# The odd token groups' gating tiles in the place of the units' first weight block, and the projection's first weight sum built there

## The chip, the cores and the metric

The kernel runs on one core of a Trainium2 chip. The metric is the time of one execution on the device in microseconds (us), the median of several runs. Engines have in-order queues: TensorE (PE in the rows) multiplies, VectorE (DVE) and ScalarE (ACT) do elementwise work, GpSimd (POOL) and SyncE (SP) issue loads and stores. A load that adds to what its target holds (an accumulating load) is issued by GpSimd.

## What is computed

A decoder layer with three token mixers, for 512 tokens of width 2048. What matters here is its second half:

```python
y_a = gmlp_branch(a_u, a_v, a_z, ...) @ w_branch_a      # u * (spatial mix of layer_norm(v)) * silu(z)
y_b = dsa_branch(...) @ w_branch_b
y_m = memory_branch(...) @ w_branch_m
merged = (sigmoid(g_a) * y_a + sigmoid(g_b) * y_b + sigmoid(g_m) * y_m)
x = x + merged @ w_out                                  # 512 x 2048 times 2048 x 2048
```

## The kernel before, in words

Every float32 product is made of three matmuls on parts: a weight tile `raw` is cast to `whi` by ScalarE (line 136), `wlo` is the rest, by VectorE (line 137), and lines 160 to 162 multiply hi by hi, hi by lo and lo by hi. A weight chunk is 256 rows by 512 columns (512 KB); its three matmuls for two or four groups of 128 tokens are 12 or 24 matmuls. Three buffers each for `whi` and `wlo` and four for `raw` set how far ahead weights come.

The gate columns g_m, g_b, g_a (and v, z before them) and the output projection are computed in **units** of 1024 columns by Strassen's scheme: seven products of half-size blocks, in the order A11, S1, S2, A12, S3, A22, N4, with weight sums in the tiles `a` (four buffers of the pool `hold`) and `b` (another four). Results wait in `ev` (four buffers) to be stored to DRAM as `kept_*`.

When the last gate unit is over, the pools `hold` and `ev` close, and `cpool` opens in their place, with the branch a operand `ya0`, `ya1` and the tiles `odd0`, `odd1`. The **gating** of branch a goes through the four groups of 128 tokens (c = 0 to 3): it loads the factors v, u, z of a group (line 938), takes statistics (989), scales (994, 996), multiplies u by z (998), mixes on TensorE (1005) and transposes into `ya` (1016). Even groups use the large pool's tiles, odd ones `odd0` and `odd1`. It runs as a task: pieces of it are issued between the weight chunks of the **branch products**, which go m, b, a for the column groups (512 columns each) 0 and 1, then m, b, a for 2 and 3. At the end of each, line 1119 multiplies the result in PSUM by its gate, which frees the bank, and 1121 adds. After branch a, `merged` is transposed (1035, 1036).

The **projection** begins with a unit of its own (`first_output_unit`), with the products in the order A11, S3, S1, S2, A12, A22, N4. Its left operands come from `merged`: A11 and S3 from the left half (`left_half`, which uses `odd1` for its differences), S1, S2 and N4 from the right half (`right_half(j)`, j = 0 and 1: column groups 2 and 3). S3's weights are B12 + B22, built in `b` by a plain load by SyncE (`b12_22`, line 1164) and an accumulating load (1174); S1's are B11 + B12, built so in `a` (1164, 1179). The pools `hold` and `ev` are open again for this, in the place of `cpool`. The second unit is the general `strassen`.

The scheduler that records the program sets each engine's order; the source gives dependences and priorities.

Of the kernel before, what the change touches and what calls it, by code (L numbers as in the profile page):

```python
# [59 lines left out]
def hybrid_block(ctx: ExitStack, tc: tile.TileContext, a, out):  # L60
# [717 lines left out]
    def held(tag):  # L778
        return pools["hold"].tile([P, CK, 512], F32, tag=tag, name=tag)
# [61 lines left out]
    def strassen(w, c0, finished, placing=None, after={}, ops=ops, before_last=None):  # L841

        wv = w.rearrange("(k p) c -> p k c", p=P)
        def load(to, kh, ch, k):
            SP.dma_start(to, wv[:, kh * 8 + k:kh * 8 + k + CK, c0 + ch * 512:c0 + ch * 512 + 512])
            return to
# [12 lines left out]
        def b11(k):  # L859
            va[k] = load(held("a"), 0, 0, k)  # L860
            parts = split_pair(va[k])
            vb[k] = load(held("b"), 0, 1, k)
            add(va[k], vb[k])
            if k == 8 - CK and placing:
                placing()
            return parts
# [68 lines left out]
    def factors_load(c, new):  # L935
        uvz[c] = two = new()
        for t, i, name in ((two[0], 0, "v"), (two[1], 0, "u"), (two[1], 1, "z")):
            G.dma_start(t[:, i, :], kept[name][:, c, :])
# [35 lines left out]

    stage = opened(("cpool", 1))
    y_of["a"] = tuple(pools["cpool"].tile([P, 8, T], F32R, tag=f"ya{n}", name=f"ya{n}") for n in range(2))
    odd8 = lambda tag="odd1": pools["cpool"].tile([P, 2, 1024], F32, tag=tag, name=tag)
    odd_two = lambda: (odd8("odd0"), odd8("odd1"))

    def gating():  # L980
        for c in range(NT):
            if c + 1 < NT and c % 2 == 0:
                factors_load(c + 1, odd_two)
# [56 lines left out]
    gops, raws, s1_first = {}, {"S2": [], "N4": []}, []  # L1040
# [28 lines left out]
    def right_half(j, s1, s2, n4):  # L1069

        a11, a21, a12, a22 = (quarter(n, j) for n in ("a11", "a21", "a12", "a22"))
        raws["S2"].append(s2)
        raws["N4"].append(n4)
        V.tensor_tensor(s1, a21, a22, op=OP.subtract)
        if j == 0:
            s1_first.append(s1)
        else:
            eighth("S1")
            for i, t in enumerate((s1_first[0], s1)):
                into("S1", i, t)  # L1080
                yield 1220
        V.tensor_tensor(s2, s1, a11, op=OP.subtract)
        V.tensor_tensor(n4, a12, s2, op=OP.add)
        yield 2440
        if j == 0:
            sixteen("A12")
            sixteen("A22")
        into("A12", j, a12)
        into("A22", j, a22)
        yield 2440  # L1090
# [8 lines left out]
    for name, cg in [(name, cg) for first in (0, 2) for name in "mba" for cg in (first, first + 1)]:  # L1099
# [26 lines left out]
        if name == "a":  # L1126
            turning = submit(turned_out(cg))
            if cg == 2:
                kept_sums = odd8("odd0")
                submit(right_half(0, quad(kept_sums[:, 0:1]), quad(kept_sums[:, 1:2]),  # L1130
                                  score_all[:, :1024].rearrange("p (k c) -> p k c", c=256)))
# [3 lines left out]
    stage = opened(("ev", 4), ("hold", 4))  # L1135
    w_out = a["w_out"]

# [20 lines left out]
    def first_output_unit():  # L1158
# [13 lines left out]
        def b12_22(k):  # L1172
            vb[k] = load(held("b"), 0, 1, k)
            G.dma_start(vb[k], block(1, 1, k), accum_op=OP.add)
            return split_pair(vb[k])
# [20 lines left out]
        e1 = ev()  # L1196
        S.copy(e1, x)
# [3 lines left out]
        n4_made = submit(parts_of("N4"))  # L1201
        e7 = ev()
        S.copy(e7, y)
        z = bank()
        block_product(gops["S1"], z, b11_12, budget=bud)
        block_product(gops["S2"], y, b11_12_22, onto=True, budget=bud)
        finish(n4_made)
        V.tensor_tensor(e1, y, e1, op=OP.add)
# [16 lines left out]
    halves = submit(right_half(1, *(quad(ev()) for _ in range(3))))  # L1225
    first_output_unit()
    strassen(w_out, 1024, given_out(1024), ops=gops, before_last=less_x(1024))
    stage.close()
    stage_s.close()
# [35 lines left out]
```

## Time and profile before

| | |
|---|---|
| median of 3 runs | 1845.69 us (1844.81 to 1846.19) |
| the profiled execution | 1846.42 us |
| its span, first to last instruction | 1844.7 us |
| TensorE busy, share of the span | 1804.9 us, 98% |
| VectorE, ScalarE busy | 1244.6 us (67%), 762.2 us (41%) |
| mean granted TensorE clock | 0.991 |
| last gate unit ends, branch products begin | 1374.48 us |
| projection begins (A11, S3, S1, S2) | 1664.65, 1688.04, 1706.00, 1720.13 us |

The span is what the trace shows; the execution's own time has 1.7 us more around it. [...]

### The profile page before, as it was taken

The numbers are of one execution on the slowest core, as the hardware profiler recorded it, in microseconds if no ns is written. First come the engines' busy times: TensorE is split into PE (matmuls) and PEld (weight loads), VectorE is DVE, ScalarE is ACT, GpSimd is POOL, SyncE is SP. The second block draws the span as 40 slices with busy tenths as digits, with TensorE's granted clock in tenths as the row PEclk, the third lists the DMA queues.
The fourth block names the chain that finished last, engine by engine and source line by source line (L and its number), as shares of the span: only waits on it lengthen the run. The fifth ranks groups of instructions, "written<-read, shape, count | busy, mean of one in ns | idle before, by whom it ended". The sixth has DMA issues, their size and how long they took to land.

```text
span 1844.7 us, 21738 instructions
## 1 busy us (share of the span) xinstructions
PE 1804.9 (98%) x8426; PEld 1508.2 (82%) x8426; DVE 1244.6 (67%) x1652; ACT 762.2 (41%) x987; POOL 114.0 (6%) x169
## 2 busy tenths in 40 slices
PE   8999999999999999999999999999998999997998
PEld 6798898888888888888888888888886888885787
DVE  8787679665446556968678686786854653455784
ACT  5744442344334354444544444444442222223443
POOL 8000000000000000000000000000111000002001
PEclk9999999999999999999999999999998999998999
DMA  7744232433332323564645646556676544338754
GB/s 229 281 126 125 70 89 78 126 115 103 94 101 69 126 69 137 184 183 130 202 147 170 185 125 204 150 169 184 221 264 219 172 151 137 126 114 242 202 167 108
DMA packets 129735, 280.95 MB, mean 152 GB/s; under 512 B 9312, under 2 KB 15456, under 8 KB 127584
## 3 DMA queue, kind: packets, MB, share of 16 engines
q1 hardware_dynamic: 111408, 211.98, 37.1%
q0 software_dynamic: 17936, 67.57, 11.2%
q8 instruction: 66, 1.08, 0.2%
q14 instruction: 37, 0.30, 0.1%
q10 hardware_dynamic: 288, 0.02, 0.0%
HBM read 248.08 MB, written 31.46 MB: 152 GB/s over the span
## 4 chain that ended last, share of the span: by engine, by line
issue 52%; PE 37%; DMA 5%; DVE 3%; POOL 2%; ACT 1%; SPq 0%; DVEq 0%; POOLq 0%; ACTq 0%
PE xyz L160 6%; PE xyz L161 6%; PE xyz L162 6%; PE acc L161 3%; PE acc L162 3%; PE acc L160 3%; DMA a<-w_out 2%; PE acc L185 1%; PE acc L186 1%; PE acc L187 1%; DVE wlo L137 1%; DMA raw<-w_branch_m 1%; DVE mTl L256 0%; PE aux L514 0%; PE aux L513 0%
## 5 line engine op out<-in xcount | busy, mean ns | idle before, releaser
L137 DVE TENSOR_TENSOR wlo<-raw,whi 128x1024 fp32r<-128x1024 f32 (+1 forms) x276 | 333.7, 1210 | 315.0 <-ACT whi L136 314.7
L136 ACT CAST whi<-raw 128x1024 fp32r<-128x1024 f32 (+1 forms) x276 | 284.2, 1031 | 556.3 <-PE xyz L162 275.7
L136 ACT CAST whi<-a 128x1024 fp32r<-128x1024 f32 x156 | 164.4, 1055 | 221.3 <-PE xyz L162 205.2
L160 PE MATMUL xyz<-whi,hTh 128*128 128x512 f32 x576 | 224.2, 389 | 0.7 <-ACT b L752 0.7
L137 DVE TENSOR_TENSOR wlo<-a,whi 128x1024 fp32r<-128x1024 f32 x156 | 188.3, 1220 | 53.9 <-ACT whi L136 53.9
L161 PE MATMUL xyz<-wlo,hTh 128*128 128x512 f32 x576 | 224.1, 389 | 0.0
L162 PE MATMUL xyz<-whi,hTl 128*128 128x512 f32 x576 | 224.1, 389 | 0.0
L160 PE MATMUL acc<-whi,hTh 128*128 128x512 f32 (+1 forms) x544 | 203.5, 374 | 0.4 <-ACT b L639 0.4
L161 PE MATMUL acc<-wlo,hTh 128*128 128x512 f32 (+1 forms) x544 | 200.8, 369 | 0.0
L162 PE MATMUL acc<-whi,hTl 128*128 128x512 f32 (+1 forms) x544 | 200.7, 369 | 0.0
L160 PEld LDWEIGHTS xyz<-whi,hTh 128*128 128x128 f32 x576 | 108.1, 188 | 23.5 <-ACT b L752 1.1
L162 PEld LDWEIGHTS xyz<-whi,hTl 128*128 128x128 f32 x576 | 108.1, 188 | 22.5
L161 PEld LDWEIGHTS xyz<-wlo,hTh 128*128 128x128 f32 x576 | 108.1, 188 | 22.4
L160 PEld LDWEIGHTS acc<-whi,hTh 128*128 128x128 f32 x544 | 102.2, 188 | 13.5 <-ACT b L639 0.8
L162 PEld LDWEIGHTS acc<-whi,hTl 128*128 128x128 f32 x544 | 102.1, 188 | 13.4
L161 PEld LDWEIGHTS acc<-wlo,hTh 128*128 128x128 f32 x544 | 102.3, 188 | 12.1
L185 PE MATMUL acc<-hTh,whi 128*128 128x512 f32 x256 | 100.1, 391 | 0.0
L186 PE MATMUL acc<-hTl,whi 128*128 128x512 f32 x256 | 99.7, 390 | 0.0
L187 PE MATMUL acc<-hTh,wlo 128*128 128x512 f32 x256 | 99.7, 389 | 0.0
L137 DVE TENSOR_TENSOR wlo<-b,whi 128x1024 fp32r<-128x1024 f32 x40 | 49.0, 1225 | 65.0 <-ACT whi L136 65.0
L852 DVE TENSOR_TENSOR a<-a,raw 128x1024 f32<-128x1024 f32 x72 | 86.4, 1220 | 0.4
L136 ACT CAST whi<-b 128x1024 fp32r<-128x1024 f32 x40 | 42.1, 1052 | 50.1 <-PE xyz L162 36.8
(363 smaller groups left out, 3530.6 us busy)
## 6 DMA issues: line engine op xcount, KB each, us to landing
raw<-w_in SPq DMA_DIRECT2D x184, 512.0 KB, 3.5
a<-w_in SPq DMA_DIRECT2D x32, 512.0 KB, 4.5
b<-w_in SPq DMA_DIRECT2D x32, 512.0 KB, 3.6
raw<-w_mem_kv SPq DMA_DIRECT2D x31, 512.0 KB, 4.5
raw<-w_out SPq DMA_DIRECT2D x28, 512.0 KB, 4.0
raw<-w_in SPq DMA_DIRECT2D x24, 368.0 KB, 3.1
raw<-w_branch_m SPq DMA_DIRECT2D x16, 512.0 KB, 5.6
raw<-w_branch_b SPq DMA_DIRECT2D x16, 512.0 KB, 3.6
```

The costliest lines, as they stand in the source:

```text
L136: S.copy(hi, src)
L137: V.tensor_tensor(lo, src, hi.bitcast(F32), op=OP.subtract)
L160: PE.matmul(ps, lhsT=lh, rhs=rh, start=first, stop=False, **k)
L161: PE.matmul(ps, lhsT=lh, rhs=rl, start=False, stop=False, **k)
L162: PE.matmul(ps, lhsT=ll, rhs=rh, start=False, stop=last, **k)
L185: PE.matmul(ps[i][:m], lhsT=hi[:, f:f + m], rhs=ah[:, k, :], start=(k == 0), stop=False)
L186: PE.matmul(ps[i][:m], lhsT=hi[:, f:f + m], rhs=al[:, k, :], start=False, stop=False)
L187: PE.matmul(ps[i][:m], lhsT=lo[:, f:f + m], rhs=ah[:, k, :], start=False, stop=(k == ktiles - 1))
L852: V.tensor_tensor(to, to, x, op=OP.add)
```

## The change

The pool with `odd0` and `odd1` opens by itself (`stage_odd`) as soon as the last unit's pools are closed, and stays open to the end. It lies where the first half of `hold`, the four `a` buffers, was; `ya0` and `ya1` lie behind it, where `b` and `ev` were. The loads for token group 1 are issued at once, ahead of the gating task. In the projection `hold` opens first, with `a` alone, at the place of `ya0`, and `ev` at that of `ya1`; `b` is no longer a tag of `hold`: `held_b` gives halves of `odd0` and `odd1`, to the first unit and, by the argument `second`, to the last one. `right_half` is taken apart: `parts_a12_a22(j)` makes the parts of A12 and A22, and `right_sums` makes the sums for S1, S2 and N4 of both halves in the four `ev` buffers, after the last branch product. The two evacuations e1 and e7, which had `ev` buffers early, come later.

```diff
@@ -838,7 +838,8 @@
         for rest in after:
             rest()
 
-    def strassen(w, c0, finished, placing=None, after={}, ops=ops, before_last=None):
+    def strassen(w, c0, finished, placing=None, after={}, ops=ops, before_last=None,
+                 second=lambda k: held("b")):
 
         wv = w.rearrange("(k p) c -> p k c", p=P)
         def load(to, kh, ch, k):
@@ -859,7 +860,7 @@
         def b11(k):
             va[k] = load(held("a"), 0, 0, k)
             parts = split_pair(va[k])
-            vb[k] = load(held("b"), 0, 1, k)
+            vb[k] = load(second(k), 0, 1, k)
             add(va[k], vb[k])
             if k == 8 - CK and placing:
                 placing()
@@ -972,15 +973,17 @@
     stage.close()
 
 
+    stage_odd = opened(("odd", 1))
+    odd8 = lambda tag="odd1": pools["odd"].tile([P, 2, 1024], F32, tag=tag, name=tag)
+    odd_two = lambda: (odd8("odd0"), odd8("odd1"))
+    factors_load(1, odd_two)
     stage = opened(("cpool", 1))
     y_of["a"] = tuple(pools["cpool"].tile([P, 8, T], F32R, tag=f"ya{n}", name=f"ya{n}") for n in range(2))
-    odd8 = lambda tag="odd1": pools["cpool"].tile([P, 2, 1024], F32, tag=tag, name=tag)
-    odd_two = lambda: (odd8("odd0"), odd8("odd1"))
 
     def gating():
         for c in range(NT):
-            if c + 1 < NT and c % 2 == 0:
-                factors_load(c + 1, odd_two)
+            if c == 2:
+                factors_load(3, odd_two)
             vo, uz = uvz.pop(c)
             u, v, o = uz[:, 0, :], vo[:, 0, :], vo[:, 1, :]
             bs = tiny.tile([P, 2, 6], F32, name="bn_s")
@@ -1037,7 +1040,7 @@
             yield 800
 
 
-    gops, raws, s1_first = {}, {"S2": [], "N4": []}, []
+    gops, raws = {}, {"S2": [], "N4": []}
 
     def eighth(name):
         gops[name] = tuple(pools["big"].tile([P, 8, 256], F32R, tag="b8", name=f"g{name}{n}") for n in "hl")
@@ -1066,28 +1069,29 @@
             into("S3", j, s3)
             yield 2440
 
-    def right_half(j, s1, s2, n4):
-
-        a11, a21, a12, a22 = (quarter(n, j) for n in ("a11", "a21", "a12", "a22"))
-        raws["S2"].append(s2)
-        raws["N4"].append(n4)
-        V.tensor_tensor(s1, a21, a22, op=OP.subtract)
-        if j == 0:
-            s1_first.append(s1)
-        else:
-            eighth("S1")
-            for i, t in enumerate((s1_first[0], s1)):
-                into("S1", i, t)
-                yield 1220
-        V.tensor_tensor(s2, s1, a11, op=OP.subtract)
-        V.tensor_tensor(n4, a12, s2, op=OP.add)
-        yield 2440
+    def parts_a12_a22(j):
         if j == 0:
             sixteen("A12")
             sixteen("A22")
-        into("A12", j, a12)
-        into("A22", j, a22)
-        yield 2440
+        for name in ("A12", "A22"):
+            into(name, j, quarter(name.lower(), j))
+            yield 1220
+
+    def right_sums():
+
+        eighth("S1")
+        temps = [quad(ev()) for _ in range(4)]
+        for j, s2, n4 in ((0, temps[1], score_all[:, :1024].rearrange("p (k c) -> p k c", c=256)),
+                          (1, temps[2], temps[3])):
+            a11, a21, a12, a22 = (quarter(n, j) for n in ("a11", "a21", "a12", "a22"))
+            V.tensor_tensor(temps[0], a21, a22, op=OP.subtract)
+            into("S1", j, temps[0])
+            V.tensor_tensor(s2, temps[0], a11, op=OP.subtract)
+            yield 3660
+            V.tensor_tensor(n4, a12, s2, op=OP.add)
+            raws["S2"].append(s2)
+            raws["N4"].append(n4)
+            yield 1220
 
     def parts_of(name):
         eighth(name)
@@ -1126,14 +1130,20 @@
         if name == "a":
             turning = submit(turned_out(cg))
             if cg == 2:
-                kept_sums = odd8("odd0")
-                submit(right_half(0, quad(kept_sums[:, 0:1]), quad(kept_sums[:, 1:2]),
-                                  score_all[:, :1024].rearrange("p (k c) -> p k c", c=256)))
+                submit(parts_a12_a22(0))
     stage.close()
 
 
-    stage = opened(("ev", 4), ("hold", 4))
+    stage = opened(("hold", 4), ("ev", 4))
     w_out = a["w_out"]
+    odds = {}
+
+    def held_b(k):
+
+        if k % (2 * CK) == 0:
+            odds[0] = odd8(f"odd{k // (2 * CK)}")
+        return odds[0][:, k // CK % 2, :].rearrange("p (a c) -> p a c", c=512)
+
 
     tiles_of = lambda t, th, c: t.rearrange("(t p) c -> p t c", p=P)[:, 2 * th:2 * th + 2, c:c + 512]
 
@@ -1170,7 +1180,7 @@
         va, vb = {}, {}
 
         def b12_22(k):
-            vb[k] = load(held("b"), 0, 1, k)
+            vb[k] = load(held_b(k), 0, 1, k)
             G.dma_start(vb[k], block(1, 1, k), accum_op=OP.add)
             return split_pair(vb[k])
 
@@ -1193,18 +1203,18 @@
         bud = 1300
         x = bank()
         block_product(gops["A11"], x, lambda k: split_pair(passing(0, 0, k)), budget=bud)
-        e1 = ev()
-        S.copy(e1, x)
         y = bank()
         block_product(gops["S3"], y, b12_22, budget=bud)
         finish(submit(parts_of("S2")))
         n4_made = submit(parts_of("N4"))
+        z = bank()
+        block_product(gops["S1"], z, b11_12, budget=bud)
         e7 = ev()
         S.copy(e7, y)
-        z = bank()
-        block_product(gops["S1"], z, b11_12, budget=bud)
         block_product(gops["S2"], y, b11_12_22, onto=True, budget=bud)
         finish(n4_made)
+        e1 = ev()
+        S.copy(e1, x)
         V.tensor_tensor(e1, y, e1, op=OP.add)
         e3 = ev()
         V.tensor_tensor(e3, z, e1, op=OP.subtract)
@@ -1222,10 +1232,12 @@
         V.tensor_tensor(e7, z, e7, op=OP.subtract)
         finished(0, 512, e7, ts=slice(0, 2))
 
-    halves = submit(right_half(1, *(quad(ev()) for _ in range(3))))
+    submit(parts_a12_a22(1))
+    submit(right_sums())
     first_output_unit()
-    strassen(w_out, 1024, given_out(1024), ops=gops, before_last=less_x(1024))
+    strassen(w_out, 1024, given_out(1024), ops=gops, before_last=less_x(1024), second=held_b)
     stage.close()
+    stage_odd.close()
     stage_s.close()
     stage_h.close()
 
```

The first place where the order of instructions moves is the end of the last gate unit. On GpSimd (`kept_a<-ev` are stores of that unit's results, `ym` and `yb` the branch operands, `b` tiles of the large pool) there stood before, from the stores on:

```order
L916 DMA kept_a<-ev 128x2x512
L927 DMA yb_10896<-y_b 128x2048
L927 DMA yb_10897<-y_b 128x2048
L916 DMA kept_a<-ev 128x2x512
L927 DMA yb_10896<-y_b 128x2048
L933 DMA b_10894<-kept_m 128x4x512
L916 DMA kept_a<-ev 128x2x512
L927 DMA yb_10897<-y_b 128x2048
L938 DMA odd_10922<-kept_v 128x1024
L938 DMA odd_10923<-kept_u 128x1024
L938 DMA odd_10923<-kept_z 128x1024
L933 DMA b_11081<-kept_b 128x4x512
```

and now:

```order
L917 DMA kept_a<-ev 128x2x512
L939 DMA odd_10768<-kept_v 128x1024
L939 DMA odd_10769<-kept_u 128x1024
L939 DMA odd_10769<-kept_z 128x1024
L928 DMA yb_10904<-y_b 128x2048
L928 DMA yb_10905<-y_b 128x2048
L917 DMA kept_a<-ev 128x2x512
L928 DMA yb_10904<-y_b 128x2048
L934 DMA b_10902<-kept_m 128x4x512
L928 DMA yb_10905<-y_b 128x2048
L917 DMA kept_a<-ev 128x2x512
L934 DMA b_11084<-kept_b 128x4x512
```

The three loads of group 1 moved ahead of the loads of `yb` and of two stores. On VectorE, the work of group 1 (`odd`) stood before behind five splits of weights (the last of N4 and four of branch m) and the evacuation of N4 (909):

```order
L222 TENSOR_TENSOR rs_r<-rs_r,rs_u 128x1
L996 SCALAR_TENSOR_TENSOR b_10664<-b_10664,rs_r,b_10645 128x1024
L137 TENSOR_TENSOR wlo<-raw,whi 128x1024 x3
L909 TENSOR_TENSOR ev<-xyz,ev 128x1024
L137 TENSOR_TENSOR wlo<-raw,whi 128x1024 x2
L989 BN_STATS bn_s<-odd_10922 128x6
L137 TENSOR_TENSOR wlo<-raw,whi 128x1024
L989 BN_STATS bn_s<-odd_10922 128x6
```

and now it begins ahead of the first of them, the split of N4's last chunk:

```order
L992 BN_STATS bn_s<-odd_10768 128x6
L221 TENSOR_SCALAR rs_u<-rs_u 128x1
L992 BN_STATS bn_s<-odd_10768 128x6
L222 TENSOR_TENSOR rs_r<-rs_r,rs_u 128x1
L1001 TENSOR_TENSOR odd_10769<-odd_10769 128x1024
L137 TENSOR_TENSOR wlo<-raw,whi 128x1024
L999 SCALAR_TENSOR_TENSOR b_10664<-b_10664,rs_r,b_10645 128x1024
L137 TENSOR_TENSOR wlo<-raw,whi 128x1024
```

The second place is the start of the projection. SyncE's loads there were, with the last two branch products ahead of them:

```order
L154 DMA raw<-w_branch_b 128x2x512 x8
L154 DMA raw<-w_branch_a 128x2x512 x8
L1164 DMA raw<-w_out 128x2x512 x8
L1164 DMA b<-w_out 128x2x512 x4
L1164 DMA a<-w_out 128x2x512 x4
```

and are now, with `odd_12725` the tile `odd0` and `odd_12772` the tile `odd1`:

```order
L1174 DMA odd_12725<-w_out 128x2x512
L154 DMA raw<-w_branch_a 128x2x512
L154 DMA raw<-w_branch_m 128x2x512 x8
L154 DMA raw<-w_branch_b 128x2x512 x8
L1174 DMA odd_12772<-w_out 128x2x512 x2
L154 DMA raw<-w_branch_a 128x2x512 x8
L1174 DMA raw<-w_out 128x2x512 x6
L1174 DMA a<-w_out 128x2x512 x4
L1174 DMA raw<-w_out 128x2x512 x2
```

The loads of the first sum moved between those of the branch products, those for `a` ahead of the last two single blocks; on GpSimd the accumulating loads (1184) moved likewise, between the gate loads. On VectorE the right half's sums (1087, 1089, 1091) and parts now stand between the splits of A11's last chunk and of S1's first (`wlo<-a`):

```order
L1087 TENSOR_TENSOR ev<-b_11650,b_12478 128x1024
L1089 TENSOR_TENSOR ev<-ev,b_11650 128x1024
L137 TENSOR_TENSOR wlo<-odd_12725,whi 128x1024
L1091 TENSOR_TENSOR score<-b_12478,ev 128x1024
L137 TENSOR_TENSOR A_12515<-b_12641,A_12515 128x1024
L137 TENSOR_TENSOR A_12516<-b_12641,A_12516 128x1024
L137 TENSOR_TENSOR gS1l<-ev,gS1h 128x1024
L137 TENSOR_TENSOR wlo<-odd_12725,whi 128x1024
L137 TENSOR_TENSOR wlo<-odd_12772,whi 128x1024
L1087 TENSOR_TENSOR ev<-b_11803,b_12641 128x1024
L137 TENSOR_TENSOR wlo<-odd_12772,whi 128x1024
L1089 TENSOR_TENSOR ev<-ev,b_11803 128x1024
```

Behind these rows come five more (`gS1l`, the last sum, `gS2l` twice, `wlo<-a`), then `gN4l` twice and the next splits for S1. Before, the first half's three sums had run earlier, beside the last branch product.

## Rows read from the trace of the kernel before

**Rows 1.** The page, part 1: busy time and share of TensorE.

```profile
PE 1804.9 (98%) x8426; PEld 1508.2 (82%) x8426; DVE 1244.6 (67%) x1652; ACT 762.2 (41%) x987; POOL 114.0 (6%) x169
```

**Rows 2.** Waits of TensorE over the span: total, times, longest, us.

```profile
PE xyz L160 <- ACT whi L136: 12.2, 2, 10.4
...
PE xyz L160 <- DVE b L1119: 6.9, 2, 6.4
```

**Rows 3.** Windows: us, busy by engine (PE first, its matmuls in brackets), clock, DMA.

```profile
1374.48:1431.70 57.22, 48.60 (x217) 39.81 (x216) 26.77 (x41) 12.96 (x15) 5.99 (x10) 0.91 0.68 246
...
1575.48:1619.00 43.52, 43.52 (x194) 36.05 (x193) 22.44 (x20) 12.31 (x12) 0.76 (x1) 1.00 0.37 120
...
1664.65:1677.45 12.80, 12.80 (x65) 10.36 (x63) 10.62 (x11) 7.99 (x11) 0.31 (x1) 1.00 0.58 190
...
1677.45:1720.13 42.68, 28.09 (x97) 20.65 (x97) 23.96 (x21) 16.13 (x16) 10.14 (x9) 0.80 1.01 265
```

**Rows 4.** Timeline of TensorE: start, duration, operation, [idle before it <- releaser].

```profile
1406.69 0.79 PE L160 MATMUL xyz<-whi,ym 128*128 128x512 f32 x1 [6.37 <-DVE b L1119]
...
1688.04 0.79 PE L160 MATMUL xyz<-whi,S 128*128 128x512 f32 x1 [10.43 <-ACT whi L136]
```

**Rows 5.** Timeline of VectorE around the last gate unit and the first branch.

```profile
1357.86 1.21 DVE L137 TENSOR_TENSOR wlo<-a,whi 128x1024 fp32r<-128x1024 f32 x1
...
1367.38 0.16 DVE L222 TENSOR_TENSOR rs_r<-rs_r,rs_u 128x1 f32<-128x1 f32 x1
...
1368.78 1.22 DVE L137 TENSOR_TENSOR wlo<-raw,whi 128x1024 fp32r<-128x1024 f32 x1
...
1382.95 1.23 DVE L137 TENSOR_TENSOR wlo<-raw,whi 128x1024 fp32r<-128x1024 f32 x1 [3.81 <-ACT whi L136]
...
1397.00 0.69 DVE L989 BATCH_NORM_STATS2 bn_s<-odd 128x6 f32<-128x512 f32 x1 [9.27 <-DMA odd<-kept_v]
...
1405.42 2.35 DVE L1119 TENSOR_TENSOR b<-b,xyz 128x1024 f32<-128x1024 f32 x2
```

**Rows 6.** The chain that ended last, 1345 to 1450 us: start, us, what.

```profile
1367.12 14.64 DMA raw<-w_branch_m
...
1391.67 5.31 DMA odd<-kept_v
```

**Rows 7.** Line 938, the factor loads: issue to landing, six loads.

```profile
DMA to landing us min/median/max: 4.3/5.5/7.3
```

**Rows 8.** Windows before and in the crowd of loads; DMA share second to last.

```profile
1358.00:1362.00 4.00, 4.00 (x19) 3.32 (x18) 3.93 (x6) 3.41 (x4) 0.67 (x1) 1.00 0.58 236
...
1362.00:1366.00 4.00, 4.00 (x19) 3.32 (x18) 4.00 (x7) 2.32 (x3) 1.09 (x2) 1.00 0.51 152
...
1366.00:1374.00 8.00, 8.00 (x37) 6.63 (x36) 5.12 (x7) 3.25 (x4) 1.28 (x2) 1.00 0.93 325
```

**Rows 9.** Timeline of VectorE around the product A11.

```profile
1669.29 1.22 DVE L137 TENSOR_TENSOR wlo<-raw,whi 128x1024 fp32r<-128x1024 f32 x1
...
1675.02 1.22 DVE L137 TENSOR_TENSOR A<-b,A 128x1024 fp32r<-128x1024 f32 x1
...
1682.97 1.22 DVE L137 TENSOR_TENSOR gN4l<-score,gN4h 128x1024 fp32r<-128x1024 f32 x1
```

**Rows 10.** Timeline of SyncE: load issues of the projection.

```profile
1670.95 2.50 SPq L1164 DMA_DIRECT2D b<-w_out  x4
...
1675.13 2.27 SPq L1164 DMA_DIRECT2D a<-w_out  x4
```

**Rows 11.** Timeline of GpSimd: the first accumulating load.

```profile
1677.14 3.76 POOL L1174 DMA_DIRECT2D b<-w_out  x3 [52.27 <-DMA b<-w_out]
```

**Rows 12.** Timeline of ScalarE: casts of the weight sums as they land.

```profile
1686.94 1.04 ACT L136 CAST whi<-b 128x1024 fp32r<-128x1024 f32 x1 [5.27 <-DMA b<-w_out]
...
1699.07 1.05 ACT L136 CAST whi<-b 128x1024 fp32r<-128x1024 f32 x1 [3.08 <-DMA b<-w_out]
...
1715.14 3.06 ACT L136 CAST whi<-a 128x1024 fp32r<-128x1024 f32 x3 [2.46 <-DMA a<-w_out]
```

## Prediction

> **What bounds the kernel now.** The page's first part comes first: TensorE is busy for 98% of the span [rows 1], so time comes only from the little that it waits, or from its clock. The list of waits says for whom: 12.2 us in two waits for a cast by ScalarE, one of them 10.4 us, and 6.9 us in two waits for line 1119 on VectorE, one of them 6.4 us [rows 2]. The timeline of TensorE places them: the first matmul of the product S3 in the output projection (1688.04), and the second column group of the first branch product (1406.69) [rows 4]. The table by windows prices both places. An undisturbed branch stretch runs its 192 matmuls in 43.52 us, 0.2267 us each, at full clock [rows 3]. The first branch product (1374.48 to 1431.70) takes 57.22 us for as many matmuls and 24 small ones. In the stretch of A11, 48 matmuls and 16 small ones take 12.80 us, so a small one takes (12.80 - 10.88) / 16 = 0.12 us, and 24 take 2.9. That leaves 57.22 - 43.52 - 2.9 = 10.8 us lost at **place one**, at a mean granted clock of 0.91. At **place two** S3 and S1, 96 matmuls worth 21.76 us, take 42.68 us: 20.9 us lost, with a clock of 0.80 (both in [rows 3]). The chain of waits and the rows of VectorE, SyncE and GpSimd then say what ends each wait.
>
> **Place one: the odd group's gating tiles.** VectorE reaches the statistics of token group 1 and idles 9.27 us for a load of its tile, until 1397.00 [rows 5]. The splits for the branch's fifth weight chunk and line 1119, which frees a PSUM bank, stand behind it in VectorE's order; line 1119 begins at 1405.42. The chain shows why the tile is late: its place belonged to the evacuation buffers, so its load (1391.67, 5.31 us) stood behind the stores out of them [rows 6].
>
> The change puts the tiles where the first weight block was. Its last reader is the last split of the product A22, over at 1357.86 + 1.21 = 1359.1 [rows 5]. The three loads can then go out at 1359.1, some 32 us earlier. Factor loads landed in 4.3 to 7.3 us [rows 7], so all three are there by 1366.4 at the latest by these rows. VectorE asks for the first just ahead of the row at 1367.38 [rows 5] and for the others a us later, so it doesn't wait. It now does, ahead of the split of N4's last chunk, two statistics (0.69 each [rows 5]) and one multiplication (1.14). That split ended at 1368.78 + 1.22 = 1370.0 [rows 5]; it will end about 2.5 us later, less the 1.3 of the scaling pass of group 0 that now comes behind it, at 1371.2. TensorE wants it at 1374.48 - 2.72 + 0.23 = 1372.0. Nothing is lost, with 0.8 us to spare. Line 1119 (now 1123) then has no late work ahead of it.
>
> What could eat this is the load traffic. The three loads, 1.5 MB, take 4.8 us at the 325 GB/s of the crowded stretch. From 1359.1 to 1366 the DMA engines are idle for (1 - 0.58) x 2.9 + (1 - 0.51) x 4 = 3.2 us, so 1.6 us of them are pushed into the crowd that follows (share 0.93; all in [rows 8]), where weights of the first branch took 14.64 us to land [rows 6]. The tightest split is that of the branch's third chunk: done at 1382.95 + 1.23 = 1384.2 [rows 5], wanted at 1374.48 + 2 x 5.44 = 1385.4, a slack of 1.2 us. If 1.6 us lands on it, 0.4 us is lost; if all 4.8 us does, 3.6. I take 0.3, nearer to the first because most of the load fits in idle time. **Place one gives 10.8 - 0.3 = 10.5 us**, between 7.2 and 10.8.
>
> **Place two: the projection's first weight sum.** S3 needs B12 + B22. Before, the loads for it were issued at 1670.95 [rows 10], after the last branch product had freed their place (1664.65) and behind eight other loads in SyncE's order; the accumulating loads followed at 1677.14 [rows 11]; the casts ran at 1686.94 to 1699.07 as the four sums landed, one every 4.0 us [rows 12]. The sum for S1 queued behind. Now all of the first sum stands in the gating tiles, free since the gating and the left half are done, during the branch products. A stretch like that has a DMA share of 0.37 [rows 3], which hides these 4 MB. SyncE's next loads wait behind the two loads of each tile, and GpSimd's gate loads behind the accumulating ones; both are used a whole column group (21.8 us) later, so a few us there cost nothing. S3 starts on time.
>
> Late next could be the sum for S1. Its loads wait only for the last branch product (1664.65) and stand ahead of the last two loads of S2. From a load's issue to its accumulating issue took 6.2 us (1670.95 to 1677.14), from there to the landing 9.8 (1677.14 to 1686.94), and 4.0 for each further one. From 1664.7 that gives 1680.7, 1684.7, 1688.7 and 1692.7. The last is wanted 2.3 us (cast and split) before its matmuls at about 1698.5. So 3.5 us is left, even at the pace of before, when twice the bytes were in the way.
>
> What then binds is VectorE. The sums of both halves now follow each other here; the three of the first half ran earlier before. By the new order, 17 operations stand from the first sum to S1's first split. Eight such follow each other in 1.14 us each (1675.02 to 1682.97 [rows 9]), and they begin behind the split of 1669.29, at 1670.4. S3's four splits are the 3rd, 8th, 9th and 11th: done by 1673.9, 1679.6, 1680.7 and 1683.0, wanted at 1677.7, 1680.4, 1683.1 and 1685.8. Cover is 0.8 us at the thinnest. S1's first is the 17th, done at 1670.4 + 16 x 1.14 + 1.22 = 1689.8, wanted at 1677.45 + 10.88 + 0.23 = 1688.6: 1.3 us lost. Its second is the 20th, done at 1693.2, wanted at 1692.6: 0.7 us. The later splits are in time. The casts and copies of ScalarE in between, some 13 at 1.05, fit in these 19 us. So S3 and S1 take 21.8 + 2.0 = 23.8 us. **Place two gives 42.68 - 23.8 = 18.9 us**, at most 20.9.
>
> [...] By 1.22 the two waits would be 2.7 and 1.0, and the sum 1.7 us worse; a step is what a queue is made of, so I go by 1.14.
>
> The two late copies out of PSUM (e1, e7) cost nothing: no product needs those banks afresh before S2 ends. Matmuls, splits and bytes are the same in number as before.
>
> **Sum.** 10.5 + 18.9 = 29.4 us. The profiled execution took 1846.42 us (span 1844.7); it would take 1817.0. The median before was 1845.69, 0.7 below it, so the forecast is **1816.3 us**. Its own range is 1814 to 1820: down to all 31.7 gained, up to the 3.6 us of place one.
>
> **Rivals.** *A. The moved loads collide.* If the odd tiles take as long as the weights in the crowd, 14.6 us, they land at 1373.7, and VectorE stands before N4's last split until then: done at 1377.4, wanted at 1372.0, 5.4 us of TensorE, and some 2 us at half clock behind such a gap (as after 1400 before). 1816.3 + 7.3 = 1823.6. Against it: the tiles leave 5 us ahead of the crowd [rows 8]. For it: a tight 0.8 us. [...] Chance 0.14.
>
> *B. The wait only moves from S3 to S1.* The last load for S1's sum was issued by 1677.4 and its cast ran at 1715.14 [rows 10, 12], 38 us on. If that were the nature of accumulating loads and not the queue of eight, the last sum would land at 1667 + 38 = 1705, and S2 begin at 1705 + 2.3 + 2.7 = 1710.0 and not 1701.2: 1816.3 + 8.8 = 1825.1. Against it: the casts 4.0 us apart, which show a queue that drains. Chance 0.12; A and B together 0.03 (1832).
>
> *C. Slower.* On SyncE the loads into the second odd tile stand ahead of all eight weight loads of the last branch product. If the left half's last split of that tile came late, every weight would wait with it. Weights there are loaded more than four chunks (21.8 us) ahead, and the left half's work stands among the splits of the product before, so the delay must pass 22 us to cost anything and 51 us to end slower than before. Chance 0.04, mostly slower.
>
> **Chances and range.** Forecast 0.67, A 0.14, B 0.12, both 0.03, C 0.04. What a measurement of this kernel can tell from no change is about 0.2%, 3.7 us; everything but C is faster by more. That gives faster 0.95, same 0.02, slower 0.03. The range goes from 1812.6 (all 31.7 us, the second wait for line 1119 of 0.5, and the 0.9 by which the fastest run lies below the median) to 1825.5, which takes in A and B alone.
>
> **What the profile after should show.** The waits of 10.4 and 6.4 us gone from TensorE's list, and no new one above 2 us; the first branch product in about 46.7 us; the odd tile's three loads issued at about 1359; S3 following A11 at once; a wait of about 1.3 us for a split at S1's second matmul; a clock of 1.00 in both stretches. I am wrong if TensorE waits in N4 of the last gate unit (A), if the cast for S1 waits for its accumulating load (B), or if weights of a branch product come late (C).

## The result, and the profile after

The changed kernel takes 1816.37 us (median of 4 runs, 1816.19 to 1816.45) against 1845.94 for the kernel before on the same chip: a ratio of 0.9841, with a 95% interval from 0.9824 to 0.9858. It is 29.6 us faster; 1816.3 was forecast. The profiled execution took 1816.45 us, with a span of 1814.7 against 1844.7.

The page's first part of the changed kernel, which answers to [rows 1]: TensorE's busy share is 99% now.

```profile
PE 1796.3 (99%) x8426; PEld 1505.0 (83%) x8426; DVE 1242.4 (68%) x1652; ACT 765.0 (42%) x989; POOL 112.2 (6%) x169
```

The waits of TensorE in the changed kernel, against [rows 2] (total, times, longest). The two waits of 10.4 and 6.4 us are gone. Line 1123 is the former line 1119.

```profile
PE xyz L161 <- DVE wlo L137: 1.8, 2, 1.5
...
PE xyz L160 <- DVE b L1123: 0.5, 1, 0.5
```

The waits for VectorE's splits were 4.5 us in six pieces in the kernel before (the row below); the two pieces that are left both stand in S1.

```profile
PE xyz L161 <- DVE wlo L137: 4.5, 6, 2.2
```

Windows of the changed kernel, against [rows 3]: the first branch product, then A11, S3, S1 and S2 (from and to, us, busy by engine, clock, DMA share, GB/s).

```profile
1374.08:1420.29 46.21, 46.21 (x217) 38.65 (x216) 23.18 (x36) 15.86 (x17) 4.41 (x7) 1.00 0.71 270
1653.20:1665.95 12.75, 12.75 (x65) 10.54 (x64) 12.63 (x12) 9.32 (x12) 4.84 (x4) 1.00 0.93 274
1665.95:1676.83 10.88, 10.88 (x49) 9.01 (x48) 10.88 (x11) 8.18 (x9) 0.00 (x0) 1.00 1.10 255
1676.83:1690.16 13.33, 11.50 (x49) 8.85 (x48) 13.33 (x13) 6.41 (x7) 0.73 (x1) 1.00 0.57 201
1690.16:1701.05 10.89, 10.89 (x50) 9.01 (x49) 10.24 (x9) 4.23 (x4) 0.00 (x0) 1.00 0.42 145
```

The branch product went from 57.22 to 46.21 us and S3 with S1 from 42.68 to 24.21: 11.0 and 18.5 us, together 29.5 of the 30.0 by which the spans differ. The granted clock is 1.00 in each stretch.

The timelines of GpSimd and VectorE at place one show why. GpSimd issues the odd tile's loads when the last split that reads the old weight block is done (the first of VectorE's rows, over at 1358.61), and VectorE, asking for them at 1366.63, has no idle time in front of its row. [rows 5] had 9.27 us there.

```profile
1358.91 0.56 POOL L939 DMA_DIRECT2D odd<-kept_v  x1 [0.64 <-DVE wlo L137]
```

```profile
1357.40 1.21 DVE L137 TENSOR_TENSOR wlo<-a,whi 128x1024 fp32r<-128x1024 f32 x1
...
1366.63 0.69 DVE L992 BATCH_NORM_STATS2 bn_s<-odd 128x6 f32<-128x512 f32 x1
...
1369.08 1.22 DVE L137 TENSOR_TENSOR wlo<-raw,whi 128x1024 fp32r<-128x1024 f32 x1
```

At place two, the rows of SyncE that answer to [rows 10]. The second half of the first sum is loaded at 1573.51, 92 us before S3 begins (1665.95), and the loads for S1's sum go out at 1653.16, as the last branch product's matmuls end (1653.20).

```profile
1573.51 0.88 SPq L1174 DMA_DIRECT2D odd<-w_out  x2
...
1653.16 1.91 SPq L1174 DMA_DIRECT2D a<-w_out  x4
```

GpSimd's accumulating loads of S1's sum, against [rows 11], and behind them their times from issue to landing.

```profile
1657.74 1.23 POOL L1189 DMA_DIRECT2D a<-w_out  x1 [44.28 <-DMA a<-w_out]
1659.16 1.21 POOL L1189 DMA_DIRECT2D a<-w_out  x1 [0.18 <-issue]
1661.42 2.48 POOL L1189 DMA_DIRECT2D a<-w_out  x2 [1.06 <-DMA a<-w_out]
```

```profile
DMA to landing us min/median/max: 9.7/11.5/14.4
```

The last of them, issued about 1662.7, has landed 14.4 us later, at 1677.1. What S1 then waits for is VectorE. These are the first of the 17 operations that the prediction counted and the 17th, S1's first split, and below them TensorE's two waits.

```profile
1658.97 1.22 DVE L1087 TENSOR_TENSOR ev<-b,b 128x1024 f32<-128x1024 f32 x1
...
1677.41 1.22 DVE L137 TENSOR_TENSOR wlo<-a,whi 128x1024 fp32r<-128x1024 f32 x1
```

```profile
1678.68 0.50 PE L161 MATMUL xyz<-wlo,gS1h 128*128 128x512 f32 x1 [1.46 <-DVE wlo L137]
1682.08 0.50 PE L161 MATMUL xyz<-wlo,gS1h 128*128 128x512 f32 x1 [0.37 <-DVE wlo L137]
```

### The profile page after: what moved, and what is told of

It reads as the page before. It is cut to its first block, busy times and chain, and to the rows that moved or that the text cites. A ratio compares the mean times of both kernels' runs of the same rounds, so it can differ in the third digit from the quotient of the medians.

```text
span 1814.7 us, 21736 instructions
## 1 busy us (share of the span) xinstructions
PE 1796.3 (99%) x8426; PEld 1505.0 (83%) x8426; DVE 1242.4 (68%) x1652; ACT 765.0 (42%) x989; POOL 112.2 (6%) x169
## 4 chain that ended last, share of the span: by engine, by line
PE 93%; DVE 3%; DMA 2%; issue 1%; ACT 1%; SPq 0%; DVEq 0%; POOL 0%; ACTq 0%
PE xyz L160 19%; PE xyz L162 19%; PE xyz L161 19%; PE acc L160 7%; PE acc L161 7%; PE acc L162 7%; PE acc L185 3%; PE acc L187 3%; PE acc L186 3%; PE aux L160 1%; DVE wlo L137 1%; PE aux L161 1%; PE aux L162 1%; PE aux L710 1%; DMA raw<-w_mem_kv 0%
## 5 line engine op out<-in xcount | busy, mean ns | idle before, releaser
L137 DVE TENSOR_TENSOR wlo<-b,whi 128x1024 fp32r<-128x1024 f32 x32 | 39.2, 1225 | 47.8 <-ACT whi L136 47.8
L161 PE MATMUL acc<-wlo,mTh 128*128 128x512 f32 x128 | 51.6, 403 | 5.8 <-DVE wlo L137 5.7
```

Of the source, the lines that this page charges most:

```text
L137: V.tensor_tensor(lo, src, hi.bitcast(F32), op=OP.subtract)
L161: PE.matmul(ps, lhsT=lh, rhs=rl, start=False, stop=False, **k)
```

## The experiments

All medians are compared with the kernel before, run beside them (1845.4 to 1846.4 us).

### The two places apart

**part_one_alone** is the kernel before with the odd tiles in a place of their own up to the projection:

```
+    stage_odd = opened(("odd", 1))
+    odd8 = lambda tag="odd1": pools["odd"].tile([P, 2, 1024], F32, tag=tag, name=tag)
+    odd_two = lambda: (odd8("odd0"), odd8("odd1"))
+    factors_load(1, odd_two)
     stage = opened(("cpool", 1))
...
     stage.close()
+    stage_odd.close()
     stage = opened(("ev", 4), ("hold", 4))
```

> The kernel before with place one alone: the first odd gating tiles lie where the units' first weight block was; the projection is left as it was. Theory (the two parts act in places 250 us apart and add up): 1845.9 less the 11.0 us that the m stretch became shorter in the changed kernel, so 1834.9 us, from 1834.0 to 1835.8; TensorE's wait on the split in N4 and the wait on the weights behind it are gone, and the projection's S3 and S1 still take about 42.7 us. Rival (the gain of place one is partly paid for by work that the new projection hides, or comes from it): outside 1833 to 1837 us.

Measured: 1829.11 us (1828.56 to 1829.74), ratio 0.9911 [0.9896, 0.9926]. That is 16.5 us faster, not 11, so the theory that the parts add up fell. The branch product is as short as in the change (46.21 us, from 1374.59 to 1420.80); the rest comes from the projection. Its windows (A11, S3, S1, S2; the wait for S3's first matmul counts to the row of A11):

```profile
1653.85:1669.38 15.53, 12.92 (x66) 10.36 (x64) 7.07 (x8) 6.21 (x9) 6.02 (x5) 1.00 0.96 285
1669.38:1685.70 16.32, 13.75 (x49) 9.87 (x49) 12.19 (x11) 8.89 (x10) 3.60 (x3) 0.90 1.10 262
1685.70:1701.62 15.92, 11.88 (x50) 8.96 (x49) 11.63 (x11) 8.19 (x9) 0.74 (x1) 1.00 0.84 219
1701.62:1714.33 12.71, 11.18 (x50) 8.93 (x49) 12.71 (x12) 4.96 (x5) 0.00 (x0) 1.00 0.52 171
```

The four products take 60.48 us. In the kernel before they took 66.37, from 1664.65 to the end of its row for S2:

```profile
1720.13:1731.02 10.89, 10.89 (x50) 9.01 (x49) 10.42 (x9) 4.22 (x4) 0.00 (x0) 1.00 0.16 53
```

So 5.9 us of the projection come with a move of tiles that the projection's code doesn't mention. SyncE's timeline shows a difference: b's loads go at 1653.81, when the last branch product ends (1653.85). Six raw loads stand ahead of them in its order where the kernel before has eight, the last two of them in this row:

```profile
1646.42 4.89 SPq L1167 DMA_DIRECT2D raw<-w_out  x2
1653.81 1.90 SPq L1167 DMA_DIRECT2D b<-w_out  x4
```

In the kernel before, the row ahead of [rows 10] ends with the seventh and eighth. The eighth waited for a raw buffer until 1670.5, 5.9 us after the branch product's end:

```profile
1644.37 26.53 SPq L1164 DMA_DIRECT2D raw<-w_out  x6
```

**part_two_alone** takes the projection and its sums from the change, and leaves the odd tiles on the evacuation buffers' place:

```
+    in_ya = [pools["cpool"].tile([P, 8, 512], F32, tag=f"ya{n}", name=f"in_ya{n}") for n in range(2)]
...
+    held = lambda tag: place(0)
...
+    ev = lambda: place(1)
```

> The kernel before with place two alone: the odd gating tiles lie on the evacuation buffers' place as before and stay open through the projection, whose first weight sum is built in them beside the last branch product; the sums on VectorE are regrouped as in the change. Theory (parts add up): 1845.9 less the 18.5 us that S3 and S1 became shorter, so 1827.4 us, from 1826.3 to 1828.5, with the waits of 10.4 and 6.4 us in the m stretch still there. Rival (the early part was needed for it): outside 1825 to 1830 us.

Measured: 1826.54 us (1825.56 to 1827.18), ratio 0.9896 [0.9882, 0.9911]. As the theory said: the four products take 47.83 us, as with the change (47.85), and the wait for line 1123 at the second column group of the branch product is still there:

```profile
1406.49 0.79 PE L160 MATMUL xyz<-whi,ym 128*128 128x512 f32 x1 [5.70 <-DVE b L1123]
```

The two parts alone gain 16.5 and 19.1 us, and together 29.6: they share 6 us.

### What the shared 6 us are

**b_loads_on_pool** and **raw_loads_on_act** both start from the kernel before and change queues alone. The first takes b's loads out from behind the raw loads, the second the raw loads from ahead of b's:

```
         def b12_22(k):
-            vb[k] = load(held("b"), 0, 1, k)
+            vb[k] = held("b")
+            G.dma_start(vb[k], block(0, 1, k))
             G.dma_start(vb[k], block(1, 1, k), accum_op=OP.add)
```

```
         def b11_12_22(k):
-            V.tensor_tensor(va[k], va[k], passing(1, 1, k), op=OP.add)
+            c = wpool.tile([P, CK, 512], F32, tag="raw", name="raw", bufs=4)
+            S.dma_start(c, block(1, 1, k))
+            V.tensor_tensor(va[k], va[k], c, op=OP.add)
```

> The kernel before with one change: the four plain loads of the first weight sum go out from GpSimd's queue instead of SyncE's, where they stood behind the fifth to eighth raw weight load. Theory (the 6 us by which place one alone came out better than its own stretch is b's loads, which no longer stood behind raw loads that wait for a raw buffer): the loads go when the last branch product is done at 1664.7, not at 1671.0, b's first sum lands near 1679 instead of 1687, and the time is 1839 to 1841.5 us. Rival (it was VectorE's or the evacuation buffers' new place): 1845 us or more.

Measured: 1845.08 us (1843.81 to 1846.15), ratio 0.9999 [0.9989, 1.0009]. No change, which by itself speaks for the rival, but the edit was not clean. S3's first wait did fall, from 10.43 us [rows 4] to 6.39. But GpSimd issued three of the plain loads at once, then three accumulating ones that each wait for a landing, and only then the fourth plain load. The fourth chunk's accumulating load went at 1687.90, and S3 waited 5.95 us for it. The run left the question open.

```profile
1663.08 2.12 POOL L1174 DMA_DIRECT2D b<-w_out  x3 [40.25 <-PE xyz L162]
...
1673.22 1.20 POOL L1174 DMA_DIRECT2D b<-w_out  x1
...
1687.90 1.20 POOL L1175 DMA_DIRECT2D b<-w_out  x1 [0.83 <-DMA b<-w_out]
```

```profile
1700.70 0.79 PE L160 MATMUL xyz<-whi,S 128*128 128x512 f32 x1 [5.95 <-ACT whi L136]
```

> The kernel before with one change: the four raw weight loads that S2 adds in (the fifth to eighth in SyncE's queue, two of which went out ahead of b's loads and waited there for a raw buffer) go out from ScalarE's queue. VectorE's order is that of before. Unlike in b_loads_on_pool all four loads of b can then go together. Theory (part of S3's wait before is that b's loads stood behind these raw loads): b's loads go near 1664.7 instead of 1671.0, its last sum lands near 1691 instead of 1699, and S1 ends 4 to 7 us earlier: 1838.5 to 1841.5 us. Rival (b's loads could not go earlier, or the time is lost to VectorE's order): 1844 us or more.

Measured: 1839.57 us (1839.0 to 1842.41), ratio 0.9966 [0.9954, 0.9978]: 6.4 us faster, as the theory said. b's loads go when the last branch product ends (1666.22 here), and S3's first wait is 5.10 us where it was 10.43 [rows 4]. The profiled execution was the slowest of the six (1842.41 us); in it the four products take 60.78 us, 5.6 less than the 66.37 of the kernel before.

```profile
1645.94 6.41 SPq L1164 DMA_DIRECT2D raw<-w_out  x2
1666.41 1.90 SPq L1164 DMA_DIRECT2D b<-w_out  x4
```

```profile
1684.23 0.80 PE L160 MATMUL xyz<-whi,S 128*128 128x512 f32 x1 [5.10 <-ACT whi L136]
```

So some 6 us of place two could be had by SyncE's order alone. The move of the odd tiles brought a better order with it (six raw loads ahead of b's and not eight) and a gain of the same size; that the 5.9 us of part_one_alone are this and nothing else is likely from its rows but not shown. Why the loads come out in another order when the tiles move wasn't tried; what is shown is what the order costs.

### Early sum or new order on VectorE

**sums_late** closes the odd tiles' place before the projection, so that the first sum lies in the held blocks again. VectorE's order of the change stays within one instruction.

```
     stage.close()
+    stage_odd.close()
...
-            vb[k] = load(held_b(k), 0, 1, k)
+            vb[k] = load(held("b"), 0, 1, k)
```

> The changed kernel with the odd tiles given up before the projection: the first weight sum lies in the held blocks again, so its loads go out only when the last branch product is done; VectorE's regrouped order stays within one instruction. Theory (it is the early loads that take S3's wait away, not the regrouping): b's sums land where a's landed in the changed kernel, 1667 to 1677 us or up to 3 later, and a's behind them at 3 to 4 us apart, so S3 and S1 end 6 to 11 us later than with the change: 1822 to 1828 us. Rival (the regrouping on VectorE alone did it): 1816 to 1818 us.

Measured: 1828.16 us (1827.61 to 1828.35), ratio 0.9905 [0.989, 0.992]: 11.8 us slower than the change, just past the far end of the theory (1828 us); the rival is out. The loss begins with b's sum, which lands late (its cast at 1666.67, S3 at 1667.77). VectorE idles 6.47 us for that cast, and its queue is late from there on: TensorE waits 3.57 us for S1's first split, with the operations of the change's order ahead of it.

```profile
1653.02:1667.77 14.75, 12.92 (x66) 10.36 (x64) 8.21 (x9) 4.28 (x6) 7.22 (x6) 1.00 1.05 316
1667.77:1684.17 16.40, 14.89 (x48) 10.52 (x48) 13.25 (x12) 9.80 (x12) 2.41 (x2) 0.79 1.10 262
1684.17:1700.76 16.59, 13.02 (x49) 10.19 (x49) 13.24 (x13) 9.79 (x10) 0.74 (x1) 0.90 0.81 213
1700.76:1712.78 12.02, 11.18 (x49) 8.93 (x48) 12.02 (x12) 4.28 (x5) 0.00 (x0) 1.00 0.48 161
```

A11 to S2 is then a ladder: 66.4 us before, 60.5 with part one alone (where SyncE's order is better), 59.8 with VectorE's new order and the buffers' new places too, 47.9 with the early sum. Taken in this order, the early sum is worth 11.9 of the 18.5, and the regrouping together with the new places 0.7; what either would be worth in another order wasn't tried.

### The margin at place one

**moved_twice** issues the three loads of the first odd group twice into the same tiles.

```
-            G.dma_start(t[:, i, :], kept[name][:, c, :])
+            for _ in range(2 if c == 1 else 1):
+                G.dma_start(t[:, i, :], kept[name][:, c, :])
```

> The changed kernel with the three loads of the first odd group issued twice in a row into the same tiles, which doubles the moved traffic from 1.5 to 3 MB and lets them land later. Theory (the weights of the m product land with some 1.3 us to spare for N4's last split, and crowding is slight): the second v lands between 1368 and 1371, so N4's last split is done between 1370.5 and 1373.5 where it is wanted at 1371.6: 0 to 2 us more than the change, 1816.4 to 1818.4 us. Rival A's mechanism (moved loads push the weights of the m product back): the weights land some 5 us later, and the time is 1820 us or more.

Measured: 1819.09 us (1817.99 to 1820.44), ratio 0.9857 [0.984, 0.9873], 2.7 us over the change and between the two expectations. The trace tells which mechanism it was. GpSimd waits until the first load of a tile has landed before it issues the second, so the second v goes out at 1363.34, 5.5 us behind the first. VectorE idles 2.74 us for it and TensorE 1.88 us for N4's last split behind it. N4 takes 14.23 us instead of 10.88, with a mean granted clock of 0.91; the branch product after it takes 46.69 us, only 0.5 more. So the run tests a late tile more than doubled traffic at one time; the 1.5 MB more did not push the weights back by an amount that counts.

```profile
1363.34 0.53 POOL L940 DMA_DIRECT2D odd<-kept_v  x1 [3.94 <-DMA odd<-kept_v]
```

```profile
1372.52 0.50 PE L161 MATMUL xyz<-wlo,N4h 128*128 128x512 f32 x1 [1.88 <-DVE wlo L137]
```

```profile
1370.05 1.29 DVE L993 BATCH_NORM_STATS2 bn_s<-odd 128x6 f32<-128x512 f32 x2 [2.74 <-DMA odd<-kept_v]
```

```profile
1362.09:1376.32 14.23, 12.35 (x50) 9.76 (x49) 11.35 (x19) 7.81 (x8) 3.38 (x6) 0.91 1.00 387
1376.32:1423.01 46.69, 46.69 (x217) 38.97 (x216) 22.52 (x34) 13.33 (x14) 4.94 (x8) 0.99 0.72 275
```

**call_as_before** puts the loading call back where the code before had it (in the gating task) and leaves the tiles where the change has them. The instructions come out in the same order on every engine.

> The changed kernel with the call that loads the first odd group put back to where it stood in the code before; only the tiles' place is the change's. The instructions stand in the same order on every engine as in the changed kernel, so each theory expects 1816.4 us within 0.3; it shows what the chip repeats, and that the place of the tiles sets when their loads go, not the place of the call. Rival (the early call matters): over 1818 us.

Measured: 1816.26 us (1815.1 to 1816.68), ratio 0.9838 [0.9823, 0.9852]. The place of the tiles moved the loads, not the place of the call.

### What binds S1

**two_more_ops** adds two operations on VectorE that leave their tiles as they are, ahead of S1's first split:

```
+        for j in range(2):
+            V.tensor_tensor(raws["S2"][j], raws["S2"][j], raws["S2"][j], op=OP.max)
         z = bank()
         block_product(gops["S1"], z, b11_12, budget=bud)
```

> The changed kernel with two more VectorE operations of 1024 columns (each S2 sum's maximum with itself, which leaves it as it is) ahead of S1's first weight split. Theory (VectorE is back to back there): 2 x 1.14 = 2.3 us more in S1, 1818.7 us, from 1818.2 to 1819.2. Rival (S1 waits for the landing of its sums): 1816.4 us, no change.

Measured: 1819.75 us (1818.55 to 1820.6), ratio 0.9855 [0.9839, 0.9872]: 3.4 us over the change, where the theory had 2.3 and the rival nothing. TensorE's wait grew from 1.46 to 3.71 us, just the 2.25 of two operations. S1 grew by 4.1 (it ends at 1694.32), since the clock fell: its mean is 0.50 and 0.70 of full speed in the two windows behind the wait.

```profile
1681.00 0.80 PE L161 MATMUL xyz<-wlo,gS1h 128*128 128x512 f32 x1 [3.71 <-DVE wlo L137]
```

```profile
1681.00:1684.00 3.00, 3.00 (x7) 2.42 (x8) 3.00 (x3) 0.00 (x0) 0.73 (x1) 0.50 0.05 11
1684.00:1688.00 4.00, 4.00 (x14) 3.12 (x14) 3.40 (x4) 1.05 (x1) 0.00 (x0) 0.70 0.41 132
1688.00:1694.32 6.32, 6.32 (x30) 5.23 (x29) 6.32 (x7) 2.11 (x2) 0.00 (x0) 1.00 0.70 242
```

**s1_split_first** goes the other way: the splits of S2's and N4's sums are no longer ahead of S1's.

```
-        finish(submit(parts_of("S2")))
-        n4_made = submit(parts_of("N4"))
+        finish(sums)
+        s2_made, n4_made = submit(parts_of("S2")), submit(parts_of("N4"))
         z = bank()
         block_product(gops["S1"], z, b11_12, budget=bud)
+        finish(s2_made)
```

> The changed kernel with the splits of S2's and N4's sums taken from ahead of S1's weight splits and given out between them. Theory (the 1.9 and 0.8 us steps in S1 are VectorE's queue): S1's first split is done some 2.3 us earlier and S1 runs with 0.5 us of waits or less: 1814.0 us, from 1813.6 to 1814.8. Rival (S1 waits for the landing of its accumulated sums): 1816.4 us, no change.

Measured: 1815.56 us (1814.36 to 1815.6), ratio 0.9833 [0.9819, 0.9848], between the two. S1 did become 2.3 us shorter (11.06), but S2 0.9 us longer (11.80): its first split now comes late by 0.63 us of idle on TensorE, with three additions of line 1193 and N4's splits ahead of it on VectorE.

```profile
1666.47:1677.35 10.88, 10.88 (x49) 9.01 (x48) 10.88 (x11) 7.70 (x8) 0.00 (x0) 1.00 1.10 256
1677.35:1688.41 11.06, 11.06 (x50) 8.94 (x48) 11.06 (x11) 6.88 (x7) 0.73 (x1) 1.00 0.51 182
1688.41:1700.21 11.80, 11.17 (x50) 8.93 (x48) 11.80 (x11) 4.21 (x4) 0.00 (x0) 1.00 0.54 186
```

**n4_splits_last** takes N4's splits behind the S2 product too:

```
-        s2_made, n4_made = submit(parts_of("S2")), submit(parts_of("N4"))
+        s2_made = submit(parts_of("S2"))
...
         block_product(gops["S2"], y, b11_12_22, onto=True, budget=bud)
-        finish(n4_made)
+        finish(submit(parts_of("N4")))
```

> The kernel of s1_split_first with the two splits of N4's sums put behind the S2 product as well, so that VectorE's queue holds 12 operations instead of 14 from S1's first split to S2's last. Theory (the 1.0 us step that s1_split_first showed at S2's second matmul is three additions and two N4 splits ahead of S2's first split): S2's second split is done some 2.5 us before it is wanted, S1 and S2 together take 21.8 to 22.2 us instead of 24.2 with the change, and the time is 1814.0 us, from 1813.5 to 1814.7. Rival (the sums' landings or ScalarE come next): 1815.2 us or more.

> The changed kernel once more, for comparison in the same stretch of runs: 1816.3 us, from 1815.8 to 1816.8.

Measured: 1814.20 us (1813.85 to 1815.07), ratio 0.9831 [0.9817, 0.9846], and for the change in the same stretch of runs 1816.52 (1815.71 to 1816.8), ratio 0.9842 [0.9828, 0.9857]. The intervals against the kernel before overlap, but the runs of the two do not, and the trace agrees: S1 and S2 take 21.97 us instead of 24.22, with no wait left in them. This version beats both kernels, by 2.3 us over the change.

```profile
1677.09:1688.18 11.09, 11.09 (x49) 8.93 (x48) 11.09 (x11) 6.89 (x7) 0.00 (x0) 1.00 0.54 199
1688.18:1699.06 10.88, 10.88 (x49) 9.01 (x48) 10.88 (x10) 4.23 (x4) 0.73 (x1) 1.00 0.47 163
```

## Why the prediction was right

**Place one.** Forecast 10.5 us, measured 11.0. The loads left at 1358.91 (forecast 1359.1), VectorE did not wait for them, and N4's last split was over at 1370.3, where 1371.2 was forecast; 0.4 of this is that the whole stretch came so much earlier in this execution. TensorE wanted it at 1371.6, so 1.3 us were left (forecast 0.8). The 0.3 us held back for colliding traffic were not needed. One reading was short: the three loads go out 0.5 us apart (1358.91, 1359.46, 1359.98), so that by [rows 7] the last could have landed as late as 1367.3 and not 1366.4. VectorE multiplies u by z only at 1367.94, so nothing hung on it. moved_twice bears out the shape of rival A, though: when the tile does come late, VectorE stands before N4's split and the clock falls behind the gap (a mean of 0.91 in N4), and 2.74 us of VectorE's idle time cost 2.7 us. The change lies on the safe side of that by the 1.3 us. The second three loads took 6.7 to 8.3 us from issue to landing, against 4.8 to 6.4 for the three in the change; they go out in a stretch with a DMA share of 1.00 (1362.09 to 1376.32). What the moved loads and the weights do to each other in the DMA engines is not shown beyond these times.

**Place two.** Forecast 23.8 us for S3 and S1, measured 24.2. S3 started on time and had no wait. The queue on VectorE was the right next bound, in mechanism and nearly in size: first operation 5.77 us after A11's start (forecast 5.75), S1's first split over 25.4 us after it (25.2), waits of 1.46 and 0.37 us (1.3 and 0.7). These idle times leave out a part: from start to start the two matmuls are 1.6 and 0.5 us later than at the pace of 0.23 (1676.83 to 1678.68, 1681.33 to 1682.08), and the step behind each is 0.33. That makes the 2.4 us by which S1's 13.33 exceed 10.88, where 2.0 were forecast. two_more_ops and n4_splits_last moved this wait up and down by the operations put in or taken out. The step from start to start was 18.44 / 16 = 1.15 us. The duration of one such operation is 1.22 us in [rows 9]. Taken as the step, it would put the split 1.1 us later, by estimate (16 x 0.07); the measured step decides.

**Rival B** is out: the last sum of S1 landed at 1677.1, 23.9 us after A11's start, where the bound of 1692.7 stood 28.1 after it (at 1664.65). With the first sum out of the way, the four came within 9.7 us of each other, and the first was issued sooner after the branch product. **Rival C** is out: the weights of the last branch product came in time, and no wait stands there.

**The sum and what the experiments add.** 29.4 us were forecast and 29.6 measured. That it is so close is in part luck: place one came out 0.5 us better than forecast and place two 0.4 worse. What the prediction did not see is how place two's gain divides. It named both causes, the place that came free late and "eight other loads in SyncE's order", and priced them together. raw_loads_on_act shows that a better order of SyncE's loads by itself is worth some 6 us, and part_one_alone that moving the odd tiles brings 5.9 of the 18.5 us even with the projection untouched. The two places, 250 us apart, were added up as if they were independent; they are not. The forecast of both together came out right because the part that they share was counted once, under place two.

## What to carry to other kernels

When an address is given to another tile, look at the order of every DMA queue and not only at the tiles that were moved: a load whose place is free may stand behind one that waits for a buffer (b's loads stood so until 1670.95 in the kernel before, 6.3 us past the branch product's end). Ahead of a product that will start at once, count the operations on the engine that feeds it, and put those that a later product needs behind its splits. When a stall is taken away, price the next engine by its step from start to start over the whole queue; here that gave the new wait to half a microsecond.

## What the runs showed of the hardware

In moved_twice and two_more_ops a gap on TensorE cost more than its length, with a granted clock that fell in it or behind it; in the change and in part_one_alone the clock stayed, and the gap's length alone does not tell them apart. An idle time of 1.46 us (the change) left S1 at 1.00, and so did one of 2.84 us in part_one_alone:

```profile
1689.04 0.50 PE L161 MATMUL xyz<-wlo,gS1h 128*128 128x512 f32 x1 [2.84 <-DVE wlo L137]
```

In moved_twice behind an idle time of 1.88 us that ended at 1372.52, the matmuls of 512 columns start about 0.23 us apart up to 1373.78 and 0.43 apart from 1374.18 on. The mean clock of 0.91 and 0.99 in its two windows puts the stretch at 0.50 from about 1373.8 to 1377.2, by estimate; N4 took 3.35 us more than in the change. In two_more_ops the mean was 0.88 in the 3.6 us ahead of 1680.50, most of them idle, and 0.50 behind the 3.71 us until about 1686.4, 5.4 us long (from the 0.50 and 0.70 of the windows, by estimate); there a wait longer by 2.25 us made the product longer by 4.1.

Accumulating loads of 512 KB took 7.7 to 10.4 us from issue to landing for the first sum of the change and 9.7 to 14.4 for S1's four, of which all four were under way at once. In the kernel before, where the two sums followed each other closely, they took 9.8 to 17.8 and 19.6 to 22.6. Plain loads of the same size into S1's tiles landed in 3.9 to 7.7 in the change. Two accumulated sums that stood in one queue set the starts of S3 and S1 in the kernel before: TensorE waited 10.43 and 1.78 us there for casts, and ScalarE 5.27 and 4.78 us for the loads.
